# First group of a chunked scan: a decay chain ahead of the first activations, tanh ahead of the state recurrence, other buffers for two convolutions, and a broadcast of 4 DMAs issued later

## The chip, the cores and the metric

The kernel runs on one core of a Trainium2 chip. The metric is the time of one execution on the device in microseconds, as the median of several runs; a profiled execution gives the rows that are quoted below. In the rows PE is TensorE, PEld its weight loads, DVE VectorE, ACT ScalarE, POOL GpSimd, and SP the engine whose queue issues most DMAs ("SPq" rows are its DMA issues). Each engine works through its own instructions in order and waits for others through semaphores.

## The reference

One layer of a hybrid decoder, float32, for 512 prompt tokens and 8 sampled tokens together (T = 520 columns):

```
h    = rmsnorm(x) * (1 + sc1) + sh1                 # sc1, sh1 from silu(c) @ w_ada ("adaLN")
proj = h @ w_in                                     # u | z | x, B, C (4096 columns) | dt | gates
xBC  = silu(causal_conv4(xBC) + b)                  # depthwise, width 4, earlier rows from state_conv
dt   = softplus(dt_raw + dt_bias);  A = -exp(A_log)
# scan in 4 chunks of 128 tokens, 8 groups of 4 heads:
Acs  = cumsum(dt * A) within a chunk
y    = (C.B^T * exp(Acs_l - Acs_s), lower triangle) @ (x*dt)  +  C * exp(Acs) @ h_prev
h    = h * exp(Acs_last) + (B * exp(Acs_last - Acs))^T @ (x*dt)
y    = rmsnorm((y + D*x) * silu(z)) @ w_ssd_proj    # then gates, merge with the pooling branch, w_out, FFN
```

The sampled tokens use their own recurrent states, and need `dt` and `exp(dt*A)` spread over the channels (the tile `dtx`).

## The kernel before, in words

Activations lie as channels on partitions by tokens on columns. Every weight tile (128 by 1024 floats) is loaded by SP into a buffer `raw` (3 of them, L107), split by ACT into a rounded part `whi` (L116) and by DVE into the rest `wlo` (L117); a projection column is then 48 matmuls (8 slices of the depth, 3 products, 2 halves of 260 tokens, L129) into a PSUM tile `m` (2 of them) or two banks `b` (4).

**Start.** adaLN's sc1 and sh1 come in five slices: PE multiplies (L207), ACT copies the sums (L214), PE transposes them (L220), DVE adds the bias (L225) and modulates (L369). Between the second slice's multiplication and its transpose stand 4 matmuls on a tile of zeros (L491, `warm`). Beside the modulation PE already runs three columns: dt (tile 72), and x tiles 0 and 1.

**Scan stage.** For each group g of 8 the plan has `x0(g)`, `x1(g)` (two x tiles), `bb(g)` (B), `cc(g)` (C), then from group 1 on two gate columns `zz`. Steps of the group before (`scan`, a generator) are woven between them, so the scan of group 0 runs beside the columns of group 1. The written order is the order on every engine: PE, ACT, DVE, POOL, and in this stage SP too. Each x, B and C column goes through `conv(i, ...)`: ACT copies PSUM to `xb` and writes `v` = w3*column + bias (L642, L643), DVE adds the three other taps (L647), POOL adds the state's share for the sampled tokens (L655) and saves the tail (L656, L657), ACT takes the tanh `t` (L658), DVE makes `(t+1)*v` (L659: `xg`, `bt` or `ct`), POOL copies the sampled tokens out (L660: `xs_s`, `bc_s`). From L655 on this is an `end`, put on the list `late` and run by the next `flush()`, which is the next convolution's. i is 2g and 2g+1 for x, 16+g for B, 24+g for C. `conv_state` (5 operations of POOL, L608 and L610) makes the state's share `cpre` once, from `cvs`, a load.

dt's decays are a generator of four parts, `dt_parts`: PSUM to `dtmp` and an exponential on ACT; softplus and the cumulative sum `acs` on DVE (16 small operations, L559 to L570); then `dte` and `dds` and the stores to DRAM (`dacs`, `dscr`) on ACT, DVE and SP, with 4 DMAs that read `dscr` back, spread over channels (`dtx`, L585). `dec0`, the load of `dacs` broadcast over partitions for group 0 (L674, 1 MB), goes into `dtmp`'s memory, so it waits for the transposes of L618 too. The exponentials of a group (`decays`, ACT, L682 to L694) work on it; PE needs them, masked (DVE, L748 and L701), in the y matmuls (L787, L789). The recurrence over chunks is `hst`: a copy by ACT (L765), then three rounds of POOL (L767) and DVE (L769).

Of the kernel before, what the change touches and what calls it, by code (L numbers as in the profile page):

```python
# [9 lines left out]
F32 = mybir.dt.float32  # L10
# [6 lines left out]
P = 128  # L17
T = 520
TP = 512
NS = 8  # L20
# [20 lines left out]
NCST = 399  # L41
NRAW = 3
URGENT = 300
WARM = 17, 4
NFS = 3
NU = 40

# [5 lines left out]
def tile_decoder(ctx: ExitStack, tc: tile.TileContext, I: dict, O: dict):  # L53
# [110 lines left out]
    def todo(fn, *units):  # L164
        plan.append((units, fn))
# [269 lines left out]
    def start():  # L435
        sp = st
        RB = sp.tile([P, T], F32, name="RB")
        acc = sp.tile([P, T], F32, name="acc1")
        for s in range(1, len(SLICES)):
            raws.append(ada_rows(s))  # L440
        for k in range(KD):
            add_square(sp, acc, xT[:, k], 0, T, k == 0)
        nc.vector.tensor_scalar(cwh, pv[:, PV["cw"][0] : PV["cb"][1]], 0.5, None, ALU.mult)
        ends = {}

        def ada(s, ks=range(KD)):
            m0, m1 = SLICES[s]
            n, q = P, m1 - m0
            if ks[0] == 0:
                ends[s] = bank()  # L450
            for k in ks:
                ada_mm(ends[s], raws[s][:, k], k, n, k == 0, k == KD - 1, 2 * q)
            if ks[-1] == KD - 1:
                with urgent():
                    ends[s] = ada_end(ends[s], n, lambda i: (U_SC1, U_SH1)[i // q] + m0 + i % q, sp, 2 * q)

        def normed(k):
            xn = sp.tile([P, T], F32, tag="xn", name=f"xn{k}", bufs=3)
            (nc.vector if k % 2 == 0 else nc.gpsimd).tensor_tensor(xn, xT[:, k], RB, ALU.mult)
            return xn  # L460

        def modded(s):
            m0, m1 = SLICES[s]
            with urgent():
                ends[s]()
                a1 = mod[:, U_SC1 + m0 : U_SC1 + m1]
                nw = V["n1w"][:, m0:m1].unsqueeze(2).broadcast_to([P, m1 - m0, 9])
                nc.vector.scalar_tensor_tensor(a1, a1, 1.0, nw, ALU.add, ALU.mult)

        def rows(*ks):  # L470
            hs = []
            for k in ks:
                h = sp.tile([P, T], F32, tag="h", name=f"h{k}", bufs=2)
                modulate(h, xn.pop(k), mod[:, U_SC1 + k], mod[:, U_SH1 + k])
                nc.scalar.copy(hh[:, k], h)
                hs.append(h)
            for k in ks:
                if k + 2 < KD:
                    xn[k + 2] = normed(k + 2)
            for k, h in zip(ks, hs):  # L480
                nc.vector.tensor_tensor(hl[:, k], h, hh[:, k].bitcast(F32), ALU.subtract)  # L481

        def products(k, tiles=range(3)):
            for o, w in [(outs[i], ws[i]) for i in tiles]:
                product(o, w, k, hh[:, k], hl[:, k], k == 0, k == KD - 1)


        def warm(n):
            b = bank()
            for _ in range(n):  # L490
                nc.tensor.matmul(b[:, 0:256], cold[:, 0:P], cold, start=True, stop=True)  # L491

        warm(WARM[0])
        r = rstd_start(acc, 1024, range(5))
        ws = [parts(w, "st") for w in wraw[:2]]
        ada(0)
        modded(0)
        rstd_end(r, range(5), RB)
        xn = {k: normed(k) for k in range(2)}
        rows(0)  # L500
        ada(1)
        warm(WARM[1])
        modded(1)
        ws.append(parts(wraw[2], "st"))
        outs = [both(main()), both(main()), pair()]
        products(0)
        rows(1)
        ada(2)
        products(1)
        rows(2)  # L510
        modded(2)
        products(2)
        rows(3)
        ada(3)
        products(3)
        rows(4)
        modded(3)
        products(4)
        rows(5)
        ada(4)  # L520
        products(5)
        rows(6)
        modded(4)
        rows(7)
        ahead(3, 3)
        products(6)
        products(7)
        first["ps"] = outs
        closed(st_)
# [7 lines left out]
    S = {}  # L537

    def dt_parts(sp):
# [39 lines left out]
        nc.scalar.activation(dds[:, 1], dA[0:NH, 128:136], AF.Exp, bias=0.0, scale=1.0)  # L579
        dscr = dp.tile([2, NH, NS], F32, name="dscr")  # L580
        nc.sync.dma_start(out=dscr.rearrange("a h b -> h a b"), in_=dds)
        for half in range(2):
            for a in range(2):
                src = dscr[a].rearrange("(j t) b -> t j b", t=2)[half : half + 1]
                nc.sync.dma_start(out=dtx[64 * half : 64 * half + 64, a], in_=src.broadcast_to([64, NX, NS]))  # L585
        S.update(dtt=dtt, acs=acs, dte=dte, dacs=dacs)
        yield

    def ssd_open(*_):
# [11 lines left out]
    def conv_state():  # L601

        sp, cvs = S["sp"], S["cvs"]
        cpre = sp.tile([P, 32, NS], F32, name="cpre")
        ctmp = sp.tile([P, 32, NS], F32, tag="gz", name="ctmp", bufs=2)
        for k in range(3):
            w = cwh[:, 32 * k : 32 * k + 32].unsqueeze(2).broadcast_to([P, 32, NS])
            nc.gpsimd.tensor_tensor(ctmp if k else cpre, cvs[:, :, :, k], w, ALU.mult)  # L608
            if k:
                nc.gpsimd.tensor_tensor(cpre, cpre, ctmp, ALU.add)  # L610
        S.update(cpre=cpre)
# [10 lines left out]

    late = []

    def flush():
        for f in late:
            f()
        late.clear()

    def conv(i, outs, dst, keep, mix=None):  # L630


        sp = S["sp"]
        w = lambda k: cwh[:, 32 * k + i : 32 * k + i + 1]
        xb = sp.tile([P, 16 + T], F32, tag="xb", name=f"xb{i}", bufs=3)[:, 13:]
        v = sp.tile([P, T], F32, tag="v", name=f"v{i}", bufs=2)
        t = sp.tile([P, T], F32, tag="t", name=f"t{i}", bufs=2)
        nc.gpsimd.memset(xb[:, 0:3], 0.0)
        with urgent():
            for o, t0, t1 in outs:  # L640
                shape = halves if t1 - t0 == T else lambda ap: ap
                nc.scalar.copy(shape(xb[:, 3 + t0 : 3 + t1]), o)  # L642
                nc.scalar.activation(shape(v[:, t0:t1]), o, AF.Identity, bias=cwh[:, 128 + i : 129 + i], scale=w(3))  # L643
        if mix:
            next(mix)
        for k in range(3):
            nc.vector.scalar_tensor_tensor(v[:, 0:TP], xb[:, k : k + TP], w(k), v[:, 0:TP], ALU.mult, ALU.add)  # L647
            if mix:
                next(mix)
        if i == 1:  # L650
            conv_state()
        flush()

        def end():
            nc.gpsimd.tensor_tensor(v[:, TP:T], v[:, TP:T], S["cpre"][:, i], ALU.add)  # L655
            nc.gpsimd.tensor_copy(cvp[:, i], xb[:, TP : TP + 3])  # L656
            nc.gpsimd.tensor_copy(S["cvs"][:, i, :, 3], xb[:, TP + 3 : TP + 11])  # L657
            nc.scalar.activation(t, v, AF.Tanh, bias=0.0, scale=1.0)  # L658
            nc.vector.scalar_tensor_tensor(dst, t, 1.0, v, ALU.add, ALU.mult)  # L659
            nc.gpsimd.tensor_copy(keep, dst[:, TP:T])  # L660

        late.append(end)

    yg = [None] * NX

# [165 lines left out]
    def gate(w, i):  # L831

        sp = S["sp"]
        ps = column([w], Hh, Hl)
        t = sp.tile([P, T], F32, tag="t", name=f"zt{i}", bufs=2)
        gz = sp.tile([P, T], F32, tag="gz", name=f"gz{i}", bufs=2)
        with urgent():
            nc.scalar.activation(halves(t), ps[:, :, :H2], AF.Tanh, bias=0.0, scale=0.5)
            nc.vector.scalar_tensor_tensor(halves(gz), halves(t), 1.0, ps[:, :, :H2], ALU.add, ALU.mult)
        flush()  # L840
        nc.gpsimd.tensor_copy(gz_s[:, i], gz[:, TP:T])
        return gz

# [20 lines left out]
    def step(g):  # L864
        def fn():
            next(gens[g], None)

        return fn
# [37 lines left out]
    def bb(g):  # L906
        def fn(w):
            cur["bt"] = S["sp"].tile([P, T], F32, tag="bt", name=f"bt{g}")
            ps = column([w], Hh, Hl, outs=None if g else pair())
            conv(16 + g, whole(ps) if g else ps, cur["bt"], bc_s[:, g, 0], gens[g - 1] if g > 1 else None)  # L910

        return fn
# [35 lines left out]
    for g in range(NG):  # L948
# [5 lines left out]
        if g > 1:  # L954
            todo(part(g - 1))
        todo(x1(g), *([X1(g)] if g else []))
        if g == 0:
            todo(dt_more)
        elif g == 1:
            todo(step(0))  # L960
            todo(step(0))
            todo(part(0))
        else:
            todo(step(g - 1))
        todo(bb(g), BB(g))
        if g == 0:
            todo(sp_order(True))
# [31 lines left out]
        if g:  # L999
            todo(part(g))  # L1000
        else:
            todo(flush)

    todo(sp_order(False))
    todo(lambda: ordered.__exit__(None, None, None) and None)
# [178 lines left out]
    def half(kk):  # L1184
        if kk == 8:
            ada_step()
# [392 lines left out]
```

## Time and profile before

| | |
|---|---|
| median of 3 runs | 1116.95 us (1114.81 to 1117.01) |
| the profiled execution | 1115.18 us, its span 1113.4 us |
| granted TensorE clock, mean over the span | 0.986 |
| PE busy | 1074.8 us (97%) |
| DVE, ACT, POOL busy | 695.9, 463.6, 347.5 us |

A row of the timeline has start, duration, engine, line, operation, tiles, shapes and count; in square brackets stands the idle time of the engine just before it and what ended that. A row of windows has a stretch, its length, the busy time of PE, PEld, DVE, ACT and POOL (with instruction counts), the clock that TensorE was granted, the busy share of the DMA engines, and GB/s.

### The profile page before, as it was taken

The numbers are of one execution on the slowest core, as the hardware profiler recorded it, in microseconds if no ns is written. First come the engines' busy times: TensorE is split into PE (matmuls) and PEld (weight loads), VectorE is DVE, ScalarE is ACT, GpSimd is POOL, SyncE is SP. The second block draws the span as 40 slices with busy tenths as digits, with TensorE's granted clock in tenths as the row PEclk, the third lists the DMA queues.
The fourth block names the chain that finished last, engine by engine and source line by source line (L and its number), as shares of the span: only waits on it lengthen the run. The fifth ranks groups of instructions, "written<-read, shape, count | busy, mean of one in ns | idle before, by whom it ended". The sixth has DMA issues, their size and how long they took to land.

```text
span 1113.4 us, 22158 instructions
## 1 busy us (share of the span) xinstructions
PE 1074.8 (97%) x9339; PEld 1047.2 (94%) x9339; DVE 695.9 (63%) x963; ACT 463.6 (42%) x774; POOL 347.5 (31%) x498
## 2 busy tenths in 40 slices
PE   7977999999999999999999999999999999999995
PEld 6977899999999999999999999899999999999995
DVE  5675688878877798698667744646554553323332
ACT  4445664664754624655433323532222222222220
POOL 1132243333343352000000000499999950000001
PEclk9989899999999999999999999999999999999998
DMA  9426435525525433454445445276666642223212
GB/s 357 184 71 153 151 117 165 183 85 161 175 85 168 147 111 107 154 171 154 145 139 168 136 158 204 95 225 213 200 213 201 201 168 92 84 85 97 85 53 77
DMA packets 58467, 165.34 MB, mean 149 GB/s; under 512 B 10880, under 2 KB 16512, under 8 KB 57600
## 3 DMA queue, kind: packets, MB, share of 16 engines
q1 hardware_dynamic: 51712, 142.96, 39.4%
q0 software_dynamic: 6656, 20.98, 6.2%
q8 instruction: 73, 1.20, 0.4%
q14 instruction: 26, 0.21, 0.1%
HBM read 151.05 MB, written 12.86 MB: 147 GB/s over the span
## 4 chain that ended last, share of the span: by engine, by line
PE 87%; DMA 3%; DVE 3%; issue 2%; POOL 2%; ACT 2%; SPq 0%; POOLq 0%; DVEq 0%; ACTq 0%
PE m L129 76%; PE b L129 4%; PE b L787 2%; PE b L762 1%; DMA araw<-in_wad 1%; DMA raw<-in_win 1%; PE b L789 1%; PE b L301 1%; POOL xn L1241 1%; PE b L740 1%; PE b L723 1%; DMA xT<-in_xT 1%; DMA cvs<-in_sconv 1%; DVE wlo L117 0%; PE b L207 0%
## 5 line engine op out<-in xcount | busy, mean ns | idle before, releaser
L129 PE MATMUL m<-hh,whi 128*128 128x260 f32 (+1 forms) x1840 | 380.9, 287 | 7.6 <-ACT v L643 6.5
L129 PE MATMUL m<-hl,whi 128*128 128x260 f32 (+1 forms) x1840 | 374.2, 284 | 0.5 <-DVE hl L481 0.2
L129 PE MATMUL m<-hh,wlo 128*128 128x260 f32 (+1 forms) x1840 | 373.9, 283 | 0.0
L117 DVE TENSOR_TENSOR wlo<-raw,whi 128x1024 fp32r<-128x1024 f32 (+2 forms) x169 | 234.2, 1388 | 178.0 <-ACT whi L116 175.0
L116 ACT CAST whi<-raw 128x1024 fp32r<-128x1024 f32 (+2 forms) x169 | 173.1, 1027 | 358.0 <-PE m L129 240.4
L129 PEld LDWEIGHTS m<-hh,whi 128*128 128x128 f32 x1840 | 285.9, 189 | 13.8 <-ACT v L643 6.7
L129 PEld LDWEIGHTS m<-hl,whi 128*128 128x128 f32 x1840 | 285.4, 189 | 1.1 <-DVE hl L481 0.7
L129 PEld LDWEIGHTS m<-hh,wlo 128*128 128x128 f32 x1840 | 285.7, 189 | 0.0
L341 POOL TENSOR_TENSOR r<-me,mhalf 128x5 f32<-128x5 f32 (+2 forms) x6 | 6.4, 1065 | 437.9 <-DVE me L340 437.9
L647 DVE SCALAR_TENSOR_TENSOR v<-xb,cwh,v 128x512 f32<-128x512 f32 x96 | 72.4, 755 | 25.8 <-ACT v L643 18.5
L129 PE MATMUL m<-ah,whi 128*128 128x260 f32 x264 | 53.2, 283 | 0.0
L129 PE MATMUL m<-ah,wlo 128*128 128x260 f32 x264 | 53.1, 282 | 0.0
L129 PE MATMUL m<-al,whi 128*128 128x260 f32 x264 | 53.0, 282 | 0.0
L129 PE MATMUL m<-gh,whi 128*128 128x260 f32 x256 | 52.8, 288 | 0.0
L1345 DVE TENSOR_TENSOR fs<-m,fs 128x520 f32<-128x520 f32 (+2 forms) x23 | 15.5, 676 | 59.1 <-PE m L129 58.3
L129 PE MATMUL m<-gl,whi 128*128 128x260 f32 x256 | 51.3, 282 | 0.0
L129 PE MATMUL m<-gh,wlo 128*128 128x260 f32 x256 | 51.3, 282 | 0.0
L808 POOL TENSOR_TENSOR h<-h,cc 128x1024 f32<-128x1024 f32 x16 | 39.7, 2481 | 29.7 <-DMA cc<-dbc 27.7
L1332 POOL TENSOR_TENSOR ht<-bb,xds 128x512 f32<-128x512 f32 x32 | 46.7, 1460 | 2.1 <-DMA bb<-dbc 1.6
L642 ACT COPY xb<-m 128x520 f32<-128x520 f32 (+1 forms) x31 | 17.8, 575 | 65.5 <-PE m L129 65.5
L1334 POOL TENSOR_TENSOR hs<-hs,ht 128x512 f32<-128x512 f32 x32 | 44.0, 1374 | 0.8
L658 ACT ACTIVATE t<-v 128x520 f32<-128x520 f32 x32 | 20.4, 637 | 51.7 <-POOL v L655 51.7
(300 smaller groups left out, 1758.8 us busy)
## 6 DMA issues: line engine op xcount, KB each, us to landing
raw<-in_win SPq DMA_DIRECT2D x73, 512.0 KB, 4.9
raw<-in_wfi SPq DMA_DIRECT2D x44, 512.0 KB, 4.5
araw<-in_wada SPq DMA_DIRECT2D x24, 512.0 KB, 3.9
h<-in_sssm SPq DMA_DIRECT2D x16, 512.0 KB, 4.0
raw<-in_wssd SPq DMA_DIRECT2D x16, 512.0 KB, 3.4
hs<-in_sssm POOLq DMA_DIRECT2D x32, 256.0 KB, 4.1
out_ssms<-hs POOLq DMA_DIRECT2D x32, 256.0 KB, 3.4
raw<-in_wfo SPq DMA_DIRECT2D x16, 512.0 KB, 3.4
```

The costliest lines, as they stand in the source:

```text
L116: nc.scalar.copy(hi, raw)
L117: nc.vector.tensor_tensor(lo, raw, hi.bitcast(F32), ALU.subtract)
L129: nc.tensor.matmul(o, a[:, k, c0 : c0 + P], b[:, t0:t1], start=f, stop=e)
L301: nc.tensor.matmul(ps[32 * i : 32 * i + 32, 0:256], scr[:, k], w[:, 256 * i : 256 * i + 256], start=k == 0 and j == 0, stop=k == KD - 1 an ...
L642: nc.scalar.copy(shape(xb[:, 3 + t0 : 3 + t1]), o)
L647: nc.vector.scalar_tensor_tensor(v[:, 0:TP], xb[:, k : k + TP], w(k), v[:, 0:TP], ALU.mult, ALU.add)
L658: nc.scalar.activation(t, v, AF.Tanh, bias=0.0, scale=1.0)
L787: nc.tensor.matmul(o, xdt[:, c, 2 * i + h], dec[:, c, 2 * i + h], start=c == 0, stop=False)
L808: nc.gpsimd.tensor_tensor(h0, h0, cc.unsqueeze(2).broadcast_to([P, 4, 2, P]), ALU.mult)
L1332: nc.gpsimd.tensor_tensor(t, bb.unsqueeze(2).broadcast_to([P, 2, 2, P]), at(xds), ALU.mult)
L1334: nc.gpsimd.tensor_tensor(h, h, t, ALU.add)
L1345: nc.vector.tensor_tensor(view(s[:, t0:t1]), u, view(s[:, t0:t1]), ALU.mult)
```

## The change

Five edits. (1) The 4 matmuls on zeros between the second adaLN slice and its transpose are gone. (2) In group 0 DVE's part of `dt_parts` is run inside `conv(1)`, after its taps and ahead of the flush that ends `conv(0)`. (3) A convolution's end has two halves, the POOL and ACT half (up to the tanh) and the DVE half; the first now stands ahead of the generator step that `conv` weaves in (`mix`) and of the taps, so ahead of the recurrence. (4) `v` of B and C in group 0 (i = 16, 24) lies in the buffers of the gates (tag `gz`) and no longer shares the 2 buffers `v`; `conv_state`'s temporary lies in tag `cc` for that. (5) The 4 DMAs of `dtx` are a part of their own, run in group 2.

```diff
-        warm(WARM[0])
+        warm(WARM)
...
-        warm(WARM[1])
...
         nc.sync.dma_start(out=dscr.rearrange("a h b -> h a b"), in_=dds)
+        S.update(dtt=dtt, acs=acs, dte=dte, dacs=dacs)
+        yield
         for half in range(2):
             for a in range(2):
                 src = dscr[a].rearrange("(j t) b -> t j b", t=2)[half : half + 1]
                 nc.sync.dma_start(out=dtx[64 * half : 64 * half + 64, a], in_=src.broadcast_to([64, NX, NS]))
-        S.update(dtt=dtt, acs=acs, dte=dte, dacs=dacs)
         yield
...
-        ctmp = sp.tile([P, 32, NS], F32, tag="gz", name="ctmp", bufs=2)
+        ctmp = sp.tile([P, 32, NS], F32, tag="cc", name="ctmp")
...
-    def flush():
+    def flush(part):
         for f in late:
-            f()
-        late.clear()
+            f[part]()
+        if part:
+            late.clear()
...
-        v = sp.tile([P, T], F32, tag="v", name=f"v{i}", bufs=2)
+        v = sp.tile([P, T], F32, tag="gz" if i in (16, 24) else "v", name=f"v{i}", bufs=2)
...
+        if i == 1:
+            conv_state()
+        else:
+            flush(0)
         if mix:
             next(mix)
...
         if i == 1:
-            conv_state()
-        flush()
-
-        def end():
+            next(S["dt"])
+            flush(0)
+        flush(1)
+
+        def half():
             nc.gpsimd.tensor_tensor(v[:, TP:T], v[:, TP:T], S["cpre"][:, i], ALU.add)
             nc.gpsimd.tensor_copy(cvp[:, i], xb[:, TP : TP + 3])
             nc.gpsimd.tensor_copy(S["cvs"][:, i, :, 3], xb[:, TP + 3 : TP + 11])
             nc.scalar.activation(t, v, AF.Tanh, bias=0.0, scale=1.0)
+
+        def end():
             nc.vector.scalar_tensor_tensor(dst, t, 1.0, v, ALU.add, ALU.mult)
             nc.gpsimd.tensor_copy(keep, dst[:, TP:T])
-        late.append(end)
+        late.append((half, end))
...
-        if g == 0:
-            todo(dt_more)
-        elif g == 1:
+        if g == 1:
             todo(step(0))
             todo(step(0))
             todo(part(0))
-        else:
+        elif g:
             todo(step(g - 1))
+            if g == 2:
+                todo(dt_more)
```

The order on DVE, from the end of the first two convolutions' taps on. Before, `xg0` (of x tile 0) stands ahead of the 16 operations on `dtmp` and `acs`:

```order
L659 SCALAR_TENSOR_TENSOR xg0_655<-t0_658,v0_657 128x520
L559 TENSOR_SCALAR dtmp_642<-dtmp_642 128x136
L560 RECIPROCAL dtmp_642<-dtmp_642 128x136
L561 TENSOR_TENSOR dtmp_642<-dtmp_642 128x136
L562 TENSOR_TENSOR dtmp_642<-dtmp_642 128x136
L563 TENSOR_SCALAR dtmp_642<-dtmp_642 128x136
L565 SCALAR_TENSOR_TENSOR dtmp_642<-dtmp_642 128x136 x7
L566 SCALAR_TENSOR_TENSOR dtmp_642<-dtmp_642 128x136
L567 SCALAR_TENSOR_TENSOR dtmp_642<-dtmp_642 128x136
L568 TENSOR_SCALAR dtmp_642<-dtmp_642,ea_651 128x136
L570 SCALAR_TENSOR_TENSOR acs_706<-cst_75,dtmp_642 128x128
L647 SCALAR_TENSOR_TENSOR v16_760<-xb16_759,cwh_96,v16_760 128x512 x3
```

Now the same place on DVE reads:

```order
L558 TENSOR_SCALAR dtmp_637<-dtmp_637 128x136
L559 RECIPROCAL dtmp_637<-dtmp_637 128x136
L560 TENSOR_TENSOR dtmp_637<-dtmp_637 128x136
L561 TENSOR_TENSOR dtmp_637<-dtmp_637 128x136
L562 TENSOR_SCALAR dtmp_637<-dtmp_637 128x136
L564 SCALAR_TENSOR_TENSOR dtmp_637<-dtmp_637 128x136 x7
L565 SCALAR_TENSOR_TENSOR dtmp_637<-dtmp_637 128x136
L566 SCALAR_TENSOR_TENSOR dtmp_637<-dtmp_637 128x136
L567 TENSOR_SCALAR dtmp_637<-dtmp_637,ea_646 128x136
L569 SCALAR_TENSOR_TENSOR acs_695<-cst_75,dtmp_637 128x128
L667 SCALAR_TENSOR_TENSOR xg0_650<-t0_653,v0_652 128x520
L652 SCALAR_TENSOR_TENSOR v16_755<-xb16_754,cwh_96,v16_755 128x512 x3
```

The whole chain of dt now stands ahead of `xg0`; behind `xg0` nothing changes its place on DVE.

SP's queue behind the stores of dt; `raw53` here is the weight of group 1's first gate column. Before:

```order
L575 DMA dacs_778<-acs_706 128x128
L581 DMA dscr_783<-dds_780 32x2x8
L585 DMA dtx_93<-dscr_783 64x16x8 x4
L674 DMA dec0_858<-dacs_778 128x4x512
L107 DMA raw53_870<-in_win 128x1024
L107 DMA raw56_935<-in_win 128x1024
L818 DMA dbc_97<-bcs0_1032 16x128
```

Now the queue has in that place (the numbers in names count one less per load):

```order
L574 DMA dacs_773<-acs_695 128x128
L580 DMA dscr_778<-dds_775 32x2x8
L682 DMA dec0_849<-dacs_773 128x4x512
L107 DMA raw52_861<-in_win 128x1024
L107 DMA raw55_926<-in_win 128x1024
L826 DMA dbc_97<-bcs0_1023 16x128
```

The 4 DMAs of `dtx` have left the head of the queue; they stand in group 2, between the loads that were named `raw88` and `raw92` before.

ACT around the recurrence of group 0 (`hst0_0`) and the tanh of group 1's B (`t17`). Before:

```order
L116 CAST whi67_1133<-raw56_935 128x1024
L642 COPY xb25_1189<-m69_1140 128x520
L643 ACTIVATE v25_1190<-m69_1140,cwh_96 128x520
L765 COPY hst0_0_1201<-b70_1195 128x256
L658 ACTIVATE t17_1093<-v17_1092 128x520
L690 ACTIVATE aa_638<-dec0_858 128x512
L693 ACTIVATE dec0_858<-dec0_858,tok_960 128x128 x4
L694 ACTIVATE dec0_858<-dec0_858 128x512
```

Now, on ACT:

```order
L116 CAST whi66_1124<-raw55_926 128x1024
L643 COPY xb25_1180<-m68_1131 128x520
L644 ACTIVATE v25_1181<-m68_1131,cwh_96 128x520
L664 ACTIVATE t17_1084<-v17_1083 128x520
L773 COPY hst0_0_1196<-b69_1190 128x256
L698 ACTIVATE aa_633<-dec0_849 128x512
L701 ACTIVATE dec0_849<-dec0_849,tok_951 128x128 x4
L702 ACTIVATE dec0_849<-dec0_849 128x512
```

`t17` and the copy that starts the recurrence have changed places; on POOL the three operations ahead of `t17` likewise stand ahead of the recurrence's three. The same swap stands in every later group.

More of the change, by code (lines that the diff above doesn't have):

```diff
@@ L43 @@
 URGENT = 300
-WARM = 17, 4
+WARM = 17
 NFS = 3
@@ L839, in gate @@
             nc.vector.scalar_tensor_tensor(halves(gz), halves(t), 1.0, ps[:, :, :H2], ALU.add, ALU.mult)
-        flush()
+        flush(0)
+        flush(1)
         nc.gpsimd.tensor_copy(gz_s[:, i], gz[:, TP:T])
@@ L1001, in tile_decoder @@
         else:
-            todo(flush)
+            todo(lambda: flush(0))
+            todo(lambda: flush(1))
     todo(sp_order(False))
```

## The prediction

> **What bounds the kernel now.** I read the windows first, then PE's waits, then the timelines of the engines that end them.
>
> ```profile
> 130.00:240.00 110.00, 110.00 (x956) 108.12 (x955) 87.19 (x113) 59.92 (x114) 43.21 (x76) 1.00 0.49 152
> ...
> PE b L787 <- ACT dec L693: 7.3, 1, 7.3
> ...
> 75.19 0.80 PE L129 MATMUL m<-hh,whi 128*128 128x260 f32 x2 [6.47 <-ACT v L643]
> ...
> 103.94 0.40 PE L129 MATMUL m<-hh,wlo 128*128 128x260 f32 x2
> ...
> 117.13 0.80 PE L129 MATMUL m<-hh,whi 128*128 128x260 f32 x2
> ```
>
> From 130 to 240 us PE is busy in 110.00 of 110 us: what the change does to the other engines there is hidden, and only a later or earlier start of that stretch reaches the end of the kernel, one for one. Before it PE stands still twice: 6.47 us ahead of x1(1) at 75.19, and from 104.34 on for the y matmuls of group 0 (7.3 us, then the matmuls as the masks come), until the next column starts at 117.13. That start is what I forecast.
>
> The first wait comes from a chain on DVE:
>
> ```profile
> 54.01 0.18 ACT L556 ACTIVATE ea<-pv 128x1 f32<-128x1 f32 x1
> ...
> 55.78 5.05 DVE L647 SCALAR_TENSOR_TENSOR v<-xb,cwh,v 128x512 f32<-128x512 f32 x6 [2.03 <-ACT v L643]
> ...
> 64.89 0.70 DVE L659 SCALAR_TENSOR_TENSOR xg<-t,v 128x520 f32<-128x520 f32 x1 [4.05 <-ACT t L658]
> 65.51 0.23 DVE L559 TENSOR_SCALAR dtmp<-dtmp 128x136 f32<-128x136 f32 x1
> ...
> 71.41 2.30 DVE L647 SCALAR_TENSOR_TENSOR v<-xb,cwh,v 128x512 f32<-128x512 f32 x3
> 73.63 0.69 DVE L659 SCALAR_TENSOR_TENSOR xg<-t,v 128x520 f32<-128x520 f32 x1
> ...
> 74.36 0.78 ACT L643 ACTIVATE v<-m,cwh 128x520 f32<-128x520 f32 x1 [0.91 <-DVE xg L659]
> ```
>
> DVE ends the taps at 60.83, sits idle 4.05 us for a tanh, and only then runs dt's chain (65.51 to 71.41, 5.90 us). Its inputs are there from 54.2 on. ACT's v of C (74.36) waits for xg1 because both lie in the 2 buffers `v`; PE waits for that v, which empties its PSUM tile. But PE has 29 us of columns (75.19 to 104.34) before the second wait, and at that one it is early; the first wait matters only as a start of the rest.
>
> The second wait, its links in order:
>
> ```profile
> 88.94 2.05 POOL L730 TENSOR_TENSOR xde<-xdt,tok 128x512 f32<-128x512 f32 x2 [0.49 <-DVE xdt L728]
> ...
> 90.99 0.20 POOL L655 TENSOR_TENSOR v<-v,cpre 128x8 f32<-128x8 f32 x1
> ...
> 92.93 1.05 ACT L116 CAST whi<-raw 128x1024 fp32r<-128x1024 f32 x1 [7.36 <-DMA raw<-in_win]
> ...
> 95.05 0.63 ACT L658 ACTIVATE t<-v 128x520 f32<-128x520 f32 x1
> ...
> 104.78 0.37 ACT L765 COPY hst<-b 128x256 f32<-128x256 f32 x1
> ...
> 109.59 0.64 ACT L658 ACTIVATE t<-v 128x520 f32<-128x520 f32 x1 [4.43 <-POOL v L655]
> ...
> 110.26 0.70 DVE L659 SCALAR_TENSOR_TENSOR bt<-t,v 128x520 f32<-128x520 f32 x1 [0.41 <-ACT t L658]
> 110.88 0.69 DVE L748 TENSOR_TENSOR dec<-dec,cbm 128x512 f32<-128x512 f32 x1
> 112.75 1.90 DVE L748 TENSOR_TENSOR dec<-dec,cbm 128x512 f32<-128x512 f32 x3 [1.19 <-ACT dec L694]
> 114.56 1.89 DVE L701 TENSOR_TENSOR aa<-aa,ct 128x512 f32<-128x512 f32 x3
> ```
>
> ACT waits 7.36 us for a weight (raw53), so t3, whose input POOL has ready at 91.19, runs only at 95.05; all exponentials of group 0 stand behind it. Then ACT waits 4.43 us in t17, behind the recurrence's three rounds on POOL (104.78 to 109.85, 5.07 us), and holds the last exponentials up by it; DVE waits for those 1.19 us more between the masks.
>
> **The change part by part.**
>
> *The 4 matmuls on zeros (edit 1).*
>
> ```profile
> 24.34 1.99 PE L491 MATMUL b<-cold 128*128 128x256 f32 x8
> ...
> 26.17 0.27 PE L220 MATMUL b<-cst,ade 128*128 128x128 f32 x1
> ...
> 24.49 0.27 ACT L214 COPY ade<-b 128x128 f32<-128x128 f32 x1 [1.94 <-PE b L207]
> ```
>
> The transpose's input is there at 24.76, the transpose runs at 26.17: up to 1.4 us are gained, all of it if nothing else holds the start (the next slices come by DMA), nothing if the loads do. I take the middle, -0.7, since no row tells which.
>
> *dt's chain first, and B's and C's buffers (edits 2 and 4).* The chain starts at 60.83 in place of 65.51 and ends at 66.73; xg0, whose tanh is there at 64.87, follows to 67.35. v16's taps need xb16 cleared by POOL, which stands behind the copy of xs_s:
>
> ```profile
> 65.65 0.19 POOL L660 COPY xs_s<-xg 128x8 f32<-128x8 f32 x1 [1.20 <-DVE xg L659]
> ...
> 58.81 2.03 DVE L647 SCALAR_TENSOR_TENSOR v<-xb,cwh,v 128x512 f32<-128x512 f32 x2
> ```
>
> With 0.3 for those two the taps start at 67.65, and xg1 at 69.87 in place of 73.63: -3.8. Against it: the chain now runs beside POOL's `conv_state`. The row of 58.81 shows the price of one such meeting: two taps take 2.03 where three elsewhere take 2.30, so 0.5 more than 1.53. Four more operations of POOL may meet the chain, so 0 to 2.0; I take 1.0, which leaves -2.8 for everything that hangs on DVE.
> The Trainium skill, "SBUF — State Buffer", section "Who interferes with whom", says that a VectorE instruction with two SBUF inputs and a GpSimd instruction that reads SBUF exclude each other for a whole instruction; the 2.03 us agrees in kind, and blocking by turns would make it some 1.7 in place of 1.0 (an estimate), by which the sum below would not move, as the weight sets its next step.
> The buffers cost nothing that I can find: `gz` is first written by the gates, behind the y matmuls, and bt0 and ct0 are long done; ctmp's place in `cc` likewise. x1(1) starts some 3.0 earlier, at 72.2 (its wlo stands behind xg1), and PE so comes to the second wait at 101.3.
>
> *dtx later (edit 5).*
>
> ```profile
> 75.83 4.16 SPq L585 DMA_DIRECT2D dtx<-dscr  x4
> 80.09 0.94 SPq L674 DMA_DIRECT2D dec<-dacs  x1
> 81.14 4.24 SPq L107 DMA_DIRECT2D raw<-in_win  x2
> ...
> DMA to landing us min/median/max: 11.8/11.8/11.8
> ...
> 79.17 0.27 PE L618 MATMUL b<-cst,dte 128*128 128x128 f32 x1
> ```
>
> dec0 waits for the transposes (done at 79.44, 4.25 after x1(1)'s start) and for dtx's issue (to 79.99). Now only the transposes hold it: done at 72.2 + 4.25 = 76.45, so dec0 goes at 76.5, raw53 at 77.5, 3.6 earlier. It took 11.8 us to land behind dtx and dec0; without dtx less, and the shortest near row is 7.5:
>
> ```profile
> 142.82 0.84 SPq L107 DMA_DIRECT2D raw<-in_win  x2
> ...
> DMA to landing us min/median/max: 7.5/7.9/8.3
> ...
> 162.07 1.03 ACT L116 CAST whi<-raw 128x1024 fp32r<-128x1024 f32 x1
> ```
>
> So it lands between 85.0 and 89.3; neither end is nearer, and I take the middle, 87.15. t3 follows a weight by 2.12 (92.93 to 95.05): 89.3. POOL's side has it ready at 91.19 - 2.8 = 88.4, so the weight still decides by 0.9. t3 gains 95.05 - 89.3 = 5.75 (between 3.6 and 6.6 by the landing alone).
> In group 2 dtx stands between these two loads of 142.82. The second's ACT use is at 162.07, it lands by 151.6, so 10.5 us are free; dtx costs it 4.2 of issue and at most 11.8 - 7.5 = 4.3 of landing: hidden.
>
> *tanh ahead of the recurrence (edit 3).* t17 (0.54 to the next start) now precedes the copy of the recurrence: 104.78 - 5.75 + 0.54 = 99.57. Its end is 5.07 later, 104.64, instead of 109.85. ACT goes straight on with the exponentials, so the 1.19 us on DVE disappears. Behind the recurrence stand bt (0.62), four masks (0.62 + 1.81), three products (1.81), and PE's lag (114.56 + 1.89 to 117.13, less the overlap of rows: 0.76 from 116.37): 104.64 + 5.62 = 110.26 for the next column. That is -6.87. In later groups the same swap is under the cover of the busy PE; should that cover be gone, it would be worth the 0.54 against it, group by group.
>
> **Sum.** -0.7 - 6.87 = -7.6. The profiled execution is 1115.18, so 1107.6; the median of the runs is 1.8 above the profiled one, so **1109.4**. Its own bounds: with no meetings on DVE and POOL (t3 at 87.4, weight in time) 1.9 less, and the whole 1.4 of the warm matmuls: 1106.8. With the weight at 89.3 (t3 at 91.4, 2.1 more) and nothing for the warm matmuls: 1112.2.
>
> **The rivals.**
>
> *The clock stays up.* After either wait PE runs at half clock:
>
> ```profile
> 70.00:72.00 2.00, 0.00 (x0) 0.00 (x0) 1.86 (x6) 0.47 (x3) 0.00 (x0) 0.93 0.00 0
> ...
> 78.00:80.00 2.00, 2.00 (x17) 2.00 (x17) 0.89 (x2) 0.98 (x2) 0.61 (x4) 0.86 0.44 25
> ...
> 109.00:110.00 1.00, 0.00 (x0) 0.00 (x0) 0.42 (x1) 0.41 (x1) 0.82 (x4) 0.64 0.00 0
> ...
> 119.00:120.00 1.00, 1.00 (x9) 1.00 (x8) 0.97 (x2) 0.97 (x3) 1.00 (x3) 0.74 0.96 352
> ```
>
> By these shares the clock falls at 71.72 and 109.28 and is back at 78.56 and 119.52: steps of 6.84, 30.72 and 10.24, which are 2, 9 and 3 times 3.41. It falls 3.0 and 4.9 us after PE's last matmul, at a mark of this raster. The column at 117.13 so runs 2.39 us at half clock, 1.2 lost. By my sum PE stops from 101.3 to about 106, 4.6 us and no more 7.3: if no mark ends a stretch that is idle enough, those 1.2 stay with us: 1108.2. For it: 1.53 us idle before the mark at 105.87 did not drop the clock. Against it: the stretch before 71.72 held 0.4 us of matmuls and dropped it, and a stop of 4.6 leaves room for such a stretch at most places of the raster. 20%.
> The Trainium skill, "TensorE: Matmul & The Clock Gate", in its part on the HAM clock gate, has the clock halved after one idle window of about 3.4 us on a free-running raster; the steps agree, and taken strictly a stop of 4.6 would contain such a window only in about a third of the cases (an estimate).
>
> *Weight late, no gain at the start*: raw53 still takes 11.8 and DVE loses 2.0: the 1112.2 above. For it: the same dec0, 1 MB, is ahead. Against: 4 scattered DMAs are gone. 12%.
>
> *The second wait does not move.* If t3's weight lands later than 92, because dec0 (which the exponentials need as well) and not dtx fills the queue, t17's 0.54 is about what the removed 1.19 returns and only the warm matmuls count: 1116.2. It needs a landing of over 14 us; no row here is so long for that load. 8%.
>
> *Slower*: dtx between the loads of group 2 holds up the second weight by more than the 10.5 us that are free, the gain of 7.6 and the 2.2 of what can be measured, thus by over 20.3 us; every us beyond the 10.5 is one of PE's. At 21 us it would give 1109.4 + 10.5 = 1119.9. The 4.2 and 4.3 us worked out above speak against it. 5%.
>
> **How the numbers follow.** Forecast 55%, clock 20%, late weight 12%, unmoved 8%, slower 5%. The range takes in the forecast's bounds, and on the fast side the clock's 1.2 beyond its best: 1105.5 to 1112.5. 0.2% (2.2 us) is what can be told from no change: faster 0.87, same 0.08, slower 0.05.
>
> **What would show it.** dt's chain on DVE directly behind the taps at about 60, without the 4 us idle; C's v on ACT with no wait for DVE; PE's first wait at 3 to 4 us; the ACT wait for a weight before t3 down from 7.4 to a few us; t17 ahead of the recurrence's copy with no 4 us wait; the next column about 110. Wrong would be: the chain stretched to 8 us beside POOL, the weight still landing at 92, a new wait of PE after 130 us, or a start of x1(1) that does not come earlier.

## The result and the profile after

| | before | after |
|---|---|---|
| median | 1116.23 us (4 runs, 1114.81 to 1117.01) | 1108.05 us (4 runs, 1103.82 to 1108.48) |
| ratio | | 0.992, interval 0.9893 to 0.9947 |
| profiled execution, its span | 1115.18, 1113.4 | 1108.36, 1106.6 |
| column behind the first y matmuls | 117.13 | 109.58 |

It is faster by 8.2 us; the forecast was 1109.4, within 1105.5 to 1112.5. A second series on another chip gave 1107.38 us against 1116.29, ratio 0.9914 (0.9898 to 0.9931); its profile is the second of the changed kernel below.

PE's timeline in the changed kernel, with its two waits in brackets (lines have moved: L795 and L797 are the y matmuls, L644 the write of `v`):

```profile
71.47 0.51 PE L129 MATMUL m<-hh,whi 128*128 128x260 f32 x2 [3.37 <-ACT v L644]
...
100.53 0.40 PE L129 MATMUL m<-hh,wlo 128*128 128x260 f32 x2
105.39 2.46 PE L795 MATMUL b<-dec,xdt 128*64 128x128 f32 x16 [4.46 <-ACT whi L116]
107.75 1.90 PE L797 MATMUL b<-aa,hst 128*64 128x128 f32 x12
109.58 0.80 PE L129 MATMUL m<-hh,whi 128*128 128x260 f32 x2
```

And 110 us behind, as a window:

```profile
122.00:232.00 110.00, 110.00 (x956) 108.13 (x955) 87.64 (x115) 61.04 (x115) 41.34 (x75) 1.00 0.50 151
```

Both waits of PE remain, each some 3 us shorter, and the wait of 1.14 us inside the y matmuls (at 113.50 before) is gone. The name "ACT whi" for the second is not its cause: that cast belongs to a later weight; the first y matmul follows the first mask on DVE, which starts at 104.60 (below). From 122 us on PE is full again, so what was won at 109.58 is carried on: 7.55 us there, 6.8 in the span. The missing 0.7 is taken up behind the experiments.

DVE, with dt's chain (L558 to L569), then xg0, v16's taps, xg1:

```profile
59.63 0.22 DVE L558 TENSOR_SCALAR dtmp<-dtmp 128x136 f32<-128x136 f32 x1
...
61.36 0.77 DVE L561 TENSOR_TENSOR dtmp<-dtmp 128x136 f32<-128x136 f32 x1
...
62.92 2.86 DVE L564 SCALAR_TENSOR_TENSOR dtmp<-dtmp 128x136 f32<-128x136 f32 x7
...
67.14 0.67 DVE L667 SCALAR_TENSOR_TENSOR xg<-t,v 128x520 f32<-128x520 f32 x1
68.14 2.33 DVE L652 SCALAR_TENSOR_TENSOR v<-xb,cwh,v 128x512 f32<-128x512 f32 x3 [0.32 <-POOL xb L639]
70.38 0.69 DVE L667 SCALAR_TENSOR_TENSOR xg<-t,v 128x520 f32<-128x520 f32 x1
```

The idle 4 us are filled, and the chain is longer: 59.63 to 67.14 is 7.51 us, 5.90 before. xg1 ends 3.25 us earlier than before.

ACT from the weight to the recurrence:

```profile
87.01 1.05 ACT L116 CAST whi<-raw 128x1024 fp32r<-128x1024 f32 x1 [4.70 <-DMA raw<-in_win]
...
89.13 0.63 ACT L664 ACTIVATE t<-v 128x520 f32<-128x520 f32 x1
...
98.85 0.64 ACT L664 ACTIVATE t<-v 128x520 f32<-128x520 f32 x1
99.38 0.37 ACT L773 COPY hst<-b 128x256 f32<-128x256 f32 x1
```

DVE behind it:

```profile
103.99 0.69 DVE L667 SCALAR_TENSOR_TENSOR bt<-t,v 128x520 f32<-128x520 f32 x1
104.60 2.50 DVE L756 TENSOR_TENSOR dec<-dec,cbm 128x512 f32<-128x512 f32 x4
107.02 1.88 DVE L709 TENSOR_TENSOR aa<-aa,ct 128x512 f32<-128x512 f32 x3
```

t3, the tanh of group 1's second x tile, is the row of 89.13; all exponentials of group 0 stand behind it. t17 (98.85) now stands ahead of the recurrence's copy and waits for nothing. The four masks run without a gap.

SP's issues around dec0 and, later, dtx:

```profile
75.82 0.38 SPq L682 DMA_DIRECT2D dec<-dacs  x1
76.29 2.67 SPq L107 DMA_DIRECT2D raw<-in_win  x2
...
134.90 5.89 SPq L586 DMA_DIRECT2D dtx<-dscr  x4
140.89 1.26 SPq L107 DMA_DIRECT2D raw<-in_win  x1
```

The landings of the weight issued at 76.29 (raw52) and of the one at 140.89, and ACT's use of the latter:

```profile
DMA to landing us min/median/max: 10.7/10.7/10.7
...
DMA to landing us min/median/max: 5.2/5.2/5.2
```

```profile
153.90 1.03 ACT L116 CAST whi<-raw 128x1024 fp32r<-128x1024 f32 x1
```

dtx takes 5.89 us of the queue in group 2, and the weight behind it still lands at 146.1, 7.8 us ahead of its use.

### The profile page after: what moved, and what is told of

It is laid out like the page before. It is cut to its first block, busy times and chain, and to the rows that moved or that the text cites. A ratio compares the mean times of both kernels' runs of the same rounds, so it can differ in the third digit from the quotient of the medians.

```text
span 1106.6 us, 22150 instructions
## 1 busy us (share of the span) xinstructions
PE 1076.7 (97%) x9331; PEld 1047.9 (95%) x9331; DVE 695.7 (63%) x963; ACT 463.9 (42%) x774; POOL 345.5 (31%) x498
## 4 chain that ended last, share of the span: by engine, by line
PE 86%; DVE 4%; DMA 3%; ACT 2%; issue 2%; POOL 1%; SPq 0%; DVEq 0%; ACTq 0%; POOLq 0%
PE m L129 75%; PE b L129 4%; DMA raw<-in_win 2%; PE b L795 1%; PE b L207 1%; PE b L770 1%; PE b L797 1%; PE b L301 1%; DVE v L652 1%; PE b L748 1%; POOL hst L775 0%; PE b L731 0%; DVE acc L391 0%; DVE wlo L117 0%; DMA araw<-in_wada 0%
## 5 line engine op out<-in xcount | busy, mean ns | idle before, releaser
L117 DVE TENSOR_TENSOR wlo<-raw,whi 128x1024 fp32r<-128x1024 f32 (+2 forms) x169 | 231.6, 1373 | 162.6 <-ACT whi L116 159.5
L129 PEld LDWEIGHTS m<-gh,whi 128*128 128x128 f32 x256 | 39.2, 188 | 2.6 <-PE b L301 1.3
```

The lines of the kernel that those rows point to most:

```text
L117: nc.vector.tensor_tensor(lo, raw, hi.bitcast(F32), ALU.subtract)
L129: nc.tensor.matmul(o, a[:, k, c0 : c0 + P], b[:, t0:t1], start=f, stop=e)
```

## The experiments

Marks of a run can't be compared as they stand. The first convolutions' taps start at 53.7 to 57.0 us in the fourteen profiles, since the start stage takes longer in some than in others; so the table gives the distance from the taps to the column behind the first y matmuls, beside the ratio to the kernel before on the same chip. Each row is one profile; the two of the changed kernel lie 0.45 us apart, which is the least that a difference must exceed.

| run | taps | t3 | column | taps to column | ratio to before |
|---|---|---|---|---|---|
| before | 55.78 | 95.05 | 117.13 | 61.35 | |
| after, two profiles | 55.15, 54.61 | 89.13, 89.03 | 109.58, 109.49 | 54.43, 54.88 | 0.992 and 0.9914 |
| a_warm | 56.95 | 91.26 | 111.71 | 54.76 | 0.9937 (0.9924 to 0.995) |
| a_dtlate | 54.22 | 91.01 | 111.21 | 56.99 | 0.9936 (0.992 to 0.9952) |
| a_vtag | 54.39 | 90.38 | 110.84 | 56.45 | 0.9946 (0.9926 to 0.9965) |
| a_dtx | 54.73 | 91.12 | 111.58 | 56.85 | 0.9947 (0.9928 to 0.9967) |
| a_tanh | 54.93 | 88.91 | 110.98 | 56.05 | 0.9935 (0.992 to 0.995) |
| b_dtx | 54.77 | 92.37 | 114.44 | 59.67 | 0.9971 (0.9958 to 0.9985) |
| a_noconv | 53.73 | 86.38 | 106.84 | 53.11 | one run, 1106.0 us |
| n_tok | 53.97 | 87.99 | 108.45 | 54.48 | 0.9921 (0.9906 to 0.9935) |
| n_fill | 55.97 | 90.26 | 111.66 | 55.69 | 0.9912 (0.9896 to 0.9928) |
| n_fill_tok | 56.31 | 90.24 | 111.67 | 55.36 | 0.9907 (0.989 to 0.9925) |
| n_best | 54.16 | 88.00 | 108.21 | 54.05 | 0.9916 (0.9896 to 0.9936) |

### Each edit undone in the changed kernel

The matmuls on zeros back:

```
         ada(1)
+        warm(4)
         modded(1)
```

> The changed kernel with the 4 matmuls on zeros back. Theory: the change's chain (DVE, weight, ACT, recurrence) hangs on the start of the columns, so every later mark shifts alike: the second slice's transpose runs at about 26.2 us in place of 24.66, the taps of the first convolutions end 0.6 later, and the column behind the y matmuls of group 0 starts at 110.2 in place of 109.58; time +0.6 us on 1108. Rival: the loads set the start of the columns anyway; then the transpose moves, but that column stays at 109.6 within 0.2 and the time does not change.

All marks are later here, the column by 2.1 us, more than the 0.6 of the theory. But taps to column is 54.76, inside the two profiles of the changed kernel; so nothing behind the start depends on it. At the start itself the taps can be counted from the end of ACT's copy, which is the input of the transpose; the copy in the changed kernel, then in a_warm:

```profile
24.34 0.27 ACT L214 COPY ade<-b 128x128 f32<-128x128 f32 x1
...
24.77 0.27 ACT L214 COPY ade<-b 128x128 f32<-128x128 f32 x1 [2.25 <-PE b L207]
```

From there to the taps it is 30.5 us in the first profile after (24.61 to 55.15) and 31.9 in a_warm (25.04 to 56.95). Over all profiles it is 31.0, 31.0 and 31.9 in the three with these matmuls (before, b_dtx, a_warm), and without them 29.9 in seven, 30.2, 30.5, and 31.1 in n_fill and n_fill_tok, where the clock is at half until 29.0 and 29.3 us. So the matmuls cost 1.1 us at the start, between the shortest of either kind, and other delays there can hide that. The ratio can't tell: its interval overlaps that of the changed kernel.

dt's chain back behind xg0:

```
         if i == 1:
-            next(S["dt"])
             flush(0)
         flush(1)
+        if i == 1:
+            next(S["dt"])
```

> The changed kernel with DVE's part of dt's chain back behind xg0. Theory: the chain takes 5.9 us again (no POOL operation beside it) and not 7.5, the taps of v16 start at 71 in place of 68.1, the columns of group 1 start 2.9 later, so do the transposes, dec0 and the weight raw52, and the column behind the first y matmuls starts at 112.4 in place of 109.6; time +2.5 to +3. Rival: the weight's landing sets t3 whatever DVE does (the queue is free only later anyway); then the column moves by under 1 us.

DVE waits again for the tanh, and v16's taps start behind the chain:

```profile
63.70 0.70 DVE L668 SCALAR_TENSOR_TENSOR xg<-t,v 128x520 f32<-128x520 f32 x1 [4.91 <-ACT t L665]
...
70.23 2.30 DVE L652 SCALAR_TENSOR_TENSOR v<-xb,cwh,v 128x512 f32<-128x512 f32 x3
```

Taps to column grows by 2.1 to 2.6 us, near the theory's 2.8 (109.6 to 112.4) and far from the rival's 1. The weight follows DVE, through x1(1) and the transposes (dec0 issued at 77.48), as it did in the forecast.

B's and C's v back in the buffers `v`:

```
-        v = sp.tile([P, T], F32, tag="gz" if i in (16, 24) else "v", name=f"v{i}", bufs=2)
+        v = sp.tile([P, T], F32, tag="v", name=f"v{i}", bufs=2)
```

> The changed kernel with v of B and C of group 0 back in the 2 buffers `v`. Theory: ACT's v16 waits for xg0 (67.8) and v24 for xg1 again, so the taps of v16 start about 1.1 us later, x1(1) 1 to 1.6 later, and with it transposes, dec0, the weight, t3 and the column behind the y matmuls: 110.7 in place of 109.5; time +1.1. Rival: dt's chain was the whole of it; then x1(1) comes later by the wait for xg1 but the column stays within 0.3 us.

On DVE, then in the waits of ACT and PE:

```profile
68.73 2.33 DVE L652 SCALAR_TENSOR_TENSOR v<-xb,cwh,v 128x512 f32<-128x512 f32 x3 [1.44 <-ACT v L644]
```

```profile
ACT v L644 <- DVE xg L667: 4.4, 2, 3.6
...
PE m L129 <- ACT v L644: 5.2, 1, 5.2
```

ACT waits twice for an xg, DVE 1.44 us for v16, PE 5.2 for v24 in place of 3.4. Taps to column is 1.6 to 2.0 longer: more than the 1.1 of the theory, and not the rival's 0.3. Some 0.2 of it is chance: POOL's first operation met the taps here (5.03 us in place of 4.57), and xg0 came 0.24 later, counted from their start.

dtx back ahead of dec0 (its `yield` taken out, and the call in group 2), and the counterpart, dtx later as the only edit to the kernel before:

```
         S.update(dtt=dtt, acs=acs, dte=dte, dacs=dacs)
-        yield
         for half in range(2):
```

> The changed kernel with the 4 DMAs of dtx back ahead of dec0. Theory: their issue (4.2 to 5.9 us from about 72.5) holds dec0 to 77 or 78 and their packets hold the weight, which lands at about 90 in place of 87; t3 at 92 in place of 89.1, the column behind the first y matmuls at 112.5, time +2.5 to +3. Rival: the weight is slow because of dec0's 1 MB and not because of dtx; then it lands 1 to 1.5 us later and the column starts at 110.8.

> The kernel before with only the 4 DMAs of dtx issued later, in group 2. Theory: DVE's and PE's marks stay, the transposes are done at 79.4, dec0 is issued then and no longer at 80.1, the weight raw53 lands 10.7 us after its issue as in the changed kernel (11.8 before), at about 90.8 in place of 92.9, and t3 and the column behind the first y matmuls come 2.1 us earlier (115.0 in place of 117.13); time -2. Rival: the dtx DMAs only cost dec0's place in the queue; then 0.7 us. No wait of PE beside group 2's loads by either.

SP in a_dtx, with the landing of the weight behind dec0:

```profile
72.28 4.17 SPq L585 DMA_DIRECT2D dtx<-dscr  x4
76.56 1.03 SPq L681 DMA_DIRECT2D dec<-dacs  x1
77.69 3.97 SPq L107 DMA_DIRECT2D raw<-in_win  x2
...
DMA to landing us min/median/max: 11.3/11.3/11.3
```

dec0 and that landing in b_dtx:

```profile
78.89 0.39 SPq L675 DMA_DIRECT2D dec<-dacs  x1
79.36 2.02 SPq L107 DMA_DIRECT2D raw<-in_win  x2
...
DMA to landing us min/median/max: 10.9/10.9/10.9
```

Undoing costs 2.0 to 2.4 us of taps to column; alone it gains 1.7. Both are between theory and rival. They split by the marks: counted from the taps the weight is issued 1.8 us later in a_dtx than in the first profile after (77.69 - 54.73 against 76.29 - 55.15), and lands in 11.3 in place of 10.7. In b_dtx it is issued 0.8 earlier than in the kernel before (79.36 - 54.77 against 81.14 - 55.78), where the transposes come late as well, and lands in 10.9 in place of 11.8. So the place in the queue is worth 1.8 in one kernel and 0.8 in the other, and the landing 0.6 and 0.9; that dtx's packets cause the latter is likely but rests on single landings.

The half with the tanh back behind generator step and taps:

```
         if i == 1:
             conv_state()
-        else:
-            flush(0)
...
         if i == 1:
             next(S["dt"])
-            flush(0)
+        flush(0)
         flush(1)
```

> The changed kernel with a convolution's POOL and ACT half back behind the generator step and the taps. Theory: the recurrence starts 0.5 us earlier, but ACT waits over 4 us in t17 behind it, the last exponentials come later and DVE waits about 1.2 us between the masks, so that from t3 to the column behind the y matmuls it is 22.0 us again in place of 20.45; column at 111.1, time +1.5. Rival: the recurrence is the longer branch and decides alone; then the column starts 0.5 us earlier and the time is 0.5 less.

ACT's timeline and the wait of PE:

```profile
98.64 0.37 ACT L771 COPY hst<-b 128x256 f32<-128x256 f32 x1
103.44 0.64 ACT L662 ACTIVATE t<-v 128x520 f32<-128x520 f32 x1 [4.44 <-POOL v L659]
```

```profile
PE b L793 <- DVE dec L754: 1.1, 1, 1.1
```

Counted from the taps the recurrence starts 0.5 earlier than after (98.64 - 54.93 against 99.38 - 55.15), ACT then stands in t17 for 4.44 us, and the wait of 1.1 us inside the y matmuls is back. From t3 to the column it is 22.07 in place of 20.45: the 1.6 us of the theory, and 22.08 in the kernel before.

By the marks the four later edits are worth 2.3, 1.8, 2.2 and 1.4 us (against the mean 54.65 of the changed kernel), 7.7 together, where all at once give 61.35 - 54.65 = 6.7; each is measured with the others in place, so they need not add up. The ratios of each undone kernel lie 0.2 to 0.3% above the changed one's, but all their intervals overlap with its two, so the marks and not the times tell these edits apart.

### What stretched dt's chain

Only the first of conv_state's five operations stays:

```
-        for k in range(3):
+        for k in range(1):
```

> The changed kernel with only the first of conv_state's five POOL operations (the state's share of the sampled tokens is then incomplete). Theory: dt's chain on DVE takes 5.9 us in place of 7.5, since those operations stretch its instructions; POOL is through earlier, so t0 comes earlier as well and xg0 follows the chain at once; x1(1) starts 1.5 earlier and the column behind the y matmuls as much earlier (108.0). Rival: the chain's length comes from its place, or t0 sets xg0; then DVE's instructions stay at 7.5 us or the taps of v16 at their time.

```profile
58.71 0.22 DVE L558 TENSOR_SCALAR dtmp<-dtmp 128x136 f32<-128x136 f32 x1
...
60.34 0.30 DVE L561 TENSOR_TENSOR dtmp<-dtmp 128x136 f32<-128x136 f32 x1
...
60.94 2.31 DVE L564 SCALAR_TENSOR_TENSOR dtmp<-dtmp 128x136 f32<-128x136 f32 x7
...
64.62 0.67 DVE L664 SCALAR_TENSOR_TENSOR xg<-t,v 128x520 f32<-128x520 f32 x1
```

The chain takes 5.91 us in its new place. The 0.77 of L561 is 0.30 again, the seven of L564 2.31 in place of 2.86: the 1.6 us come from POOL's operations beside it. Here 0.5 of that is lost again, since the one operation left meets the taps (5.07 us in place of 4.57); counted from the taps x1(1) starts 1.1 us earlier (68.95 - 53.73 against 71.47 - 55.15), and the column 1.3 to 1.8 earlier (53.11).

### The weight earlier, and the clock

Transposes ahead of x1(1):

```
-            early = (lambda kk: tokens_dt() if kk == 3 else None) if g == 1 else None
+            early = None
+            if g == 1:
+                tokens_dt()
```

> The changed kernel with the transposes L618 ahead of x1(1)'s matmuls and not behind its first nine groups. Theory: dec0 waits for them alone, so it is issued at about 71.5 in place of 75.8, raw52 behind it lands by 83, ACT no longer waits 4.7 us for it, t3 runs when POOL has its input (87.9 in place of 89.1) and the column behind the y matmuls starts at 108.4; time -1.2 us against the changed kernel. Rival: t3 is set by POOL already, or the loads only queue earlier behind dec0's 1 MB; then the column stays at 109.6.

ACT, POOL and DVE in n_tok:

```profile
81.26 1.04 ACT L116 CAST whi<-raw 128x1024 fp32r<-128x1024 f32 x1
...
87.99 0.64 ACT L664 ACTIVATE t<-v 128x520 f32<-128x520 f32 x1 [1.01 <-POOL v L661]
...
84.73 3.03 POOL L738 TENSOR_TENSOR xde<-xdt,tok 128x512 f32<-128x512 f32 x2 [0.50 <-DVE xdt L736]
...
85.09 1.76 DVE L117 TENSOR_TENSOR wlo<-raw,whi 128x1024 fp32r<-128x1024 f32 x1
```

POOL's same row in the changed kernel:

```profile
85.68 2.04 POOL L738 TENSOR_TENSOR xde<-xdt,tok 128x512 f32<-128x512 f32 x2 [0.50 <-DVE xdt L736]
```

The weight is 4.6 us earlier, counted from the taps, and ACT no longer waits for it. But DVE now splits that weight while POOL works on xde: xde takes 3.03 in place of 2.04, DVE 1.76 in place of 1.2, and t3 waits for POOL. Taps to column is 54.48, where it was 54.43 and 54.88. The rival's outcome came, by another way than it said: POOL sets t3, and it is late by the 1.0 us of this meeting, about what was to be gained.

Matmuls of the identity in PE's wait, 36 in n_fill and n_fill_tok, 17 in n_best:

```
         for i in range(2):
+            if not g and not i:
+                fb = bank()
+                for _ in range(36):
+                    nc.tensor.matmul(fb[:, 0:P], cst[:, CI[0] : CI[1]], cst[:, CI[0] : CI[1]], start=True, stop=True)
             yb = bank()
```

> The changed kernel with 36 matmuls of the identity by itself (about 4 us, their result unused) in PE's wait ahead of the first y matmuls. Theory (the clock rival of the prediction): the clock then stays at 1.00 through the wait, the y matmuls and the column behind, the 3.4 us at half clock (109.6 to 113.0) are saved by half: time -1.7 us, column start at 109.3 to 109.6. Rival: PE is held by DVE's masks there and the column's matmuls by something else than the clock; then no change.

> Both: the transposes ahead of x1(1) and the 36 matmuls in PE's wait. Theory: the two add up, column start at 108.3 at full clock; time -2.9 against the changed kernel, ratio to before about 0.990. Rival: one of them takes the other's place (the wait is then shorter than the filling, which would push the y matmuls back by up to 0.5 us).

> The transposes ahead of x1(1), and 17 matmuls of the identity (0.228 us each by the run with 36, so 3.9 us) in PE's wait of 4.5 us. Theory: the filling ends before the first mask, the y matmuls start as early as without it, the clock stays at 1.00, and the column starts at 108.2 and runs at full clock; the ratio to before is 0.989 to 0.991. Rival: the clock's raster makes it a matter of luck, also elsewhere in the kernel (two other places near 20 and 705 us), and the difference to the changed kernel is within what the runs tell.

The windows of the changed kernel in which its clock (the third number from the right) changes:

```profile
106.00:107.00 1.00, 0.88 (x8) 0.43 (x8) 1.00 (x2) 1.00 (x2) 1.00 (x2) 0.60 0.93 307
...
113.00:114.00 1.00, 1.00 (x10) 1.00 (x10) 1.00 (x1) 0.00 (x0) 0.98 (x1) 0.98 0.08 33
```

PE in n_fill, with 36:

```profile
101.85 8.20 PE L792 MATMUL b<-cst 128*128 128x128 f32 x72
```

The clock and PE in n_best, with 17:

```profile
100.00:110.00 10.00, 8.19 (x74) 6.45 (x74) 8.99 (x15) 9.57 (x24) 4.37 (x6) 1.00 0.45 148
```

```profile
99.48 3.96 PE L792 MATMUL b<-cst 128*128 128x128 f32 x34
...
108.21 0.51 PE L129 MATMUL m<-hh,whi 128*128 128x260 f32 x2
```

In the changed kernel the clock falls at 106.2 and is back at 113.0, so the column runs 3.4 us at half clock (2.39 before). With filling it stays at 1.00 in all three. 36 are too many: they take 8.2 us and not 4, and y waits for them. 17 fit, and the column starts at 108.21 at full clock. Yet n_best's times don't show it: 1106.84 us, ratio 0.9916, against 0.9914 of the changed kernel in the series before; n_fill and n_fill_tok, at 0.9912 and 0.9907, don't stand apart from it either, and neither gains the 1.7 and 2.9 us of its theory. In this profile of n_best the clock falls once more, near 703 us, where it does not in either profile of the changed kernel; from the column to the end it is 1104.7 - 108.21 = 996.5 us, against 997.0 and 994.9. So none of these versions beats the changed kernel by what can be told.

## Why the prediction was right

- *The place.* Everything hung on the start of the column behind the first y matmuls: 110.26 less 0.7 for the start, 109.56, was forecast, and 109.58 came. That is closer than the steps deserve: misses cancelled.
- *From the place to the median.* The profiled execution was put at 1107.6 and is 1108.36. The 1.8 us that were added for the median did not hold: it lies 0.3 below the profiled execution, at 1108.05. So the forecast of 1109.4 was 1.35 too high, by two misses of opposite sign.
- *The warm matmuls, -0.7.* The profiled pair shows -0.63 at the taps (55.78 to 55.15) and a_warm no effect behind the start. Counted from the transpose's input it is -0.5 in this pair (31.0 to 30.5) and -1.1 between the shortest profiles with and without. Both lie in the bounds of 0 and 1.4; the middle of these was a choice that no row supported.
- *DVE, -2.8.* xg1 came 3.25 earlier, 0.63 of it from the start: -2.6. The collisions with the chain were sized at 1.0 and are 1.6 (a_noconv). That the sum is off by 0.2 only is luck: POOL's first operation waits for a load and here came behind the taps, which took 4.57 us in place of 5.05. The prediction also says that longer collisions leave the sum as it is, because the weight sets the next step. Its own chain says otherwise, since dec0 goes behind the transposes in x1(1), and a_noconv shows it: with a shorter chain x1(1), the weight and the column all come earlier. The chain's new place is worth 2.3 by a_dtlate, the buffers 1.8 by a_vtag, which overlap.
- *PE's first wait* was put at 3 to 4 us and x1(1) at 72.2 less 0.7: 3.37 and 71.47.
- *The weight.* dec0's release by the transposes was right: 76.5 less 0.7, measured 75.82. The landing, the middle of 7.5 and 11.8, was mis-sized: 10.7 against 9.65; half of that was made good by the issue, at 76.29 where 77.5 less 0.7 was forecast, since dec0's takes 0.38 us in place of 0.94 without dtx ahead of it. Behind dec0 the weight takes 9.8 to 11.8 us in the seven profiles where I read it, with or without dtx; the 7.5 of another place has no such broadcast directly ahead of it and was no guide. t3 so came at 89.13 and not 88.6.
- *tanh ahead.* The gain from t3 to the column was forecast as 22.08 less 20.96 (89.3 to 110.26), 1.1 us, and is 1.6 (a_tanh). Most of the 0.5 that made good for the weight is the recurrence: 99.38 to 104.07, 4.69 us in place of 5.07. That is no luck: with t17 ahead, POOL's first round starts (99.83) when DVE's tap beside it has just ended, and takes 0.61 us; in the kernel before and in a_tanh the two overlap and it takes 0.98 and 0.99.
- *dtx in group 2* is hidden, as said, with 7.8 us to spare. From 122 us to 700 PE's new waits sum to 0.2 us. The rival with the slower end did not happen.
- *The clock rival* (20%) did not happen by itself: in all ten profiles without filling whose stop ahead of y is 4.05 to 5.78 us long, the clock fell. By the Trainium skill, "TensorE: Matmul & The Clock Gate", in its part on the HAM clock gate, it needs an idle window of 3.4 us on a free raster; its raster agrees (106.2 to 113.0 is two steps of 3.41), a strictly idle window does not, since the 3.41 us ahead of the fall at 106.2 hold 0.71 us of matmuls (from 105.39 on).
- *The span* gained 6.8 and not the 7.55 of the column. Most of the 0.7 is the clock behind the column (3.4 us at half and not 2.4, 0.5 us more); the rest was not followed. The second profile after has the same column and a span of 1104.4, so this is chance: its column runs at half clock for 1.4 us only, which is 1.0 us less lost, and it lacks a wait of 1.0 us that the first has, as the kernel before does:

```profile
400.98 0.51 PE L129 MATMUL m<-plh,whi 128*128 128x260 f32 x2 [0.96 <-ACT ub L1040]
```

## What to carry to other kernels

Where an engine idles for a late input, its next independent work can be written ahead, but look at what will run beside it then: DVE's chain of 5.9 us took 1.6 more beside POOL, and an earlier weight lost its gain the same way. In a chain of several engines each link's edit pays only as far as the next late input: price it to there, and take the landing of a load from the rows behind the same predecessor. Effects of 1 to 2 us are told by marks in the trace counted from a common point, when the place of the clock's raster and one chance wait move the time by 1.0 us each.

## What the runs showed of the hardware

The granted clock falls and returns at marks 3.41 us apart whose place differs from run to run. In the first profile after it is down from 106.2 to 113.0, in the second from 104.1 to 110.9, with the same program and columns that start 0.1 us apart; spans of 1106.6 and 1104.4 go with them, of which this explains 1.0 us. In two other places it varies as well: near 20 us the clock is at half in all fourteen profiles, for 3.4 to 13.7 us, and near 705 us it falls in eight of them and not in the other six. A window need not be idle for the clock to fall: the 3.41 us ahead of the fall at 72.44 in n_tok held 1.83 us of matmuls, where 1.55 us ahead of 102.79 in the first profile after kept it up. So the busy time alone does not say which mark drops it. Matmuls of a 128x128 identity by itself, in float32, took 0.23 us each (36 in 8.2 us, two records for each), where the three transposes of L618, of the same shape with one record each, start 0.11 apart; the expected 4 us for 36 rested on the latter.
